# The operands of a Strassen MLP: residual rows turned by TensorE transposes, or read in short runs and turned in 32x32 blocks by VectorE

## The chip, the cores and the metric

One core of a Trainium2 chip. The metric is the device time of one execution in microseconds. Before the change its median over three runs is 1941.09 us (1940.94 to 1941.4).

## The reference

One layer of a decoder trunk with two mixers side by side, on 2048 tokens of 1024 features, float32 throughout. Cut to what matters:

```python
h  = rms_norm(x, attn_norm_g)
z  = h @ w_in                            # q, k, v, gate_b, gate_c, xc
y_attn = swa_sink_attention(rms_norm(q), rms_norm(k), v, sinks)   # window of 128
y_conv = gate_b * short_conv(gate_c * xc, conv_w)                 # 3 taps
x  = x + concat(rms_norm(y_attn), rms_norm(y_conv)) @ w_out
hm = rms_norm(x, mlp_norm_g)             # x / sqrt(mean(x^2) + eps) * g
x  = x + square(relu(hm @ w_up)) @ w_down        # 1024 -> 4096 -> 1024
```

The change is about `hm`: how the rows of the second `x` (called x1 in the kernel) become the operands of `hm @ w_up`.

## The kernel before, in words

**Numbers.** Each matrix operand is split into a high and a low part of a narrower float type (`F32R`), and each product is three matmuls (`mm3`, L264 to L266): high by high, high by low, low by high. A matmul contracts over the 128 partitions, so the features of `hm` must lie on the partitions, and the tokens along the row. The rows of x1 have tokens on the partitions. They have to be turned.

**Stages.** The mixers run in four chunks of 512 tokens (`mixers`). Beside the attention of a chunk, other work is issued step by step from a generator (`besides`): the convolution, the convolution half of the output projection (`out_projection` with half 1; its PSUM tiles are `pout`), and the preparation of the next chunk. The finished rows of x1 of each chunk are written to DRAM (`x1_dram`), and their factors 1/sqrt(mean + eps) stand in a small tile `rs_x1`, one column for 128 tokens. The attention half of the output projection of the last chunk comes last, in two halves of 512 columns (dh 0 and dh 1).

Then comes the MLP. It is one level of a Strassen scheme: the 1024 features and the tokens are cut in 2 x 2 blocks of 512, and seven products take the place of eight. Two token blocks are worked on: rows 0 to 1023 (token block 0) and rows 1024 to 2047 (token block 1). In each, four blocks b11, b21, b12, b22 (feature half, token half) and sums of them make the seven operands, which are kept in DRAM (`xop_dram[token block][product]`), 128 partitions by 2048 floats each. The order in which products read them is `ORDER` = 1, 2, 6, 5, 3, 7, 4. `load_x` reads an operand in two halves (L368), casts the high part on ScalarE (L369) and subtracts for the low part on VectorE (L370). The up projection's matmuls are L1401 (PSUM tile `u`), the down projection's L1508 (`d`). Up weights are loaded 8 products ahead (`PRE`), split by ScalarE and VectorE (`split_up`, L386 and L387, tile `wop`) 3 ahead (`LEAD`).

**First stage: the operands of token block 0.** `prepare_mlp` runs in `besides` of the last chunk, beside the attention, in place of the preparation of a next chunk. A tile is 128 tokens by 1024 features. For each of eight tiles, in the order of all four of the first token half and then all four of the second:

- `fetch`: one DMA of 128 rows into one of two `xt` buffers (L884), then `scaled` on VectorE: times the row's factor and times the gain row, which is a 128 x 1024 tile with the gain on all partitions (L280);
- `raised`: for each feature half, four TensorE transposes of 128 x 128 (L306) into a PSUM bank `tr`, and one copy of 128 x 512 from there to SBUF on ScalarE (L307);
- for a tile of the first token half, two stores to `xop_dram` (`x_put`, L313): operands 1 and 2; for one of the second, `x_sums`: a store for operand 3, and four subtractions on VectorE (L319) with a store each for operands 5, 6, 7 and 4.

So operands 1 and 2 are complete when the fourth tile is done. `begin_mlp` then reads operand 1, loads the first four up-weight blocks (`wu_first`, L381) and splits them. The matmuls of the MLP's first product follow in TensorE's order those of pout dh 0, and those of dh 1 come after them.

**Second stage: token block 1.** `prepare_rest` is a generator that takes one step after each MLP product of token block 0. Per tile: `fetch` (L1195), for the last chunk the row's factor (`norm_stats`), the row times its factor on VectorE (L1199); then four transposes (L1212) into `tr` and one VectorE multiplication from PSUM by the gain columns `g_cols` (L1216; features are on the partitions now, so the gain is a column); stores and subtractions as above, the subtractions on GpSimd.

**What sets the order.** The instructions of each engine run in an order that is fixed at build time. A scheduler arranges them by data dependences and by priorities: `ahead(n)` and the table `PRIO` raise the priority of a piece of work, and `FILL` says how many steps of `besides` go between pieces of attention. DMAs are issued by an engine's queue in its instruction order; nearly all loads and the `x_put` stores are issued by SyncE (SP), the stores of the MLP's hidden values by GpSimd (POOL) and ScalarE. An SP that waits for a buffer holds back what stands behind it.

Of the kernel before, what the change touches and what calls it, by code (L numbers as in the profile page):

```python
# [16 lines left out]
P = 128  # L17
# [53 lines left out]
STEPS = 3  # L71
REST = 7
# [29 lines left out]
def hymba_layer(  # L102
# [46 lines left out]
    ]  # L149
    wds_dram = [[dram.tile([P, 2, BW], F32, name=f"wds{g}_{i}") for i in range(2)] for g in range(NCG // 2)]  # L150
# [149 lines left out]
    def raised(xt, dst, name, tag="tr"):  # L300

        for k in range(2):
            pt = bank(tag, f"pt_{name}_{k}")
            for j in range(NB):
                r = slice((NB * k + j) * P, (NB * k + j + 1) * P)
                nc.tensor.transpose(pt[:, j * P : (j + 1) * P], xt[:, r], ident)  # L306
            nc.scalar.copy(dst(k), pt)  # L307
            yield

    def x_put(tb, t, i, b):  # L310

        dst = xop_dram[tb][ORDER.index(i)].rearrange("p (h t c) -> p h t c", h=2, t=NB)
        nc.sync.dma_start(dst[:, :, t], b.rearrange("p (h c) -> p h c", h=2))  # L313

    def x_sums(tb, t, b11, b21, b12, b22, t1):


        def sub(i, dst, a, b):
            nc.vector.tensor_tensor(dst, a, b, op=ALU.subtract)  # L319
            x_put(tb, t, i, dst)  # L320

        x_put(tb, t, 3, b22)
        sub(5, t1, b12, b11)
        sub(6, b11, b22, t1)
        sub(7, b12, b22, b12)
        sub(4, b21, b21, b11)

# [186 lines left out]
    with tc.tile_pool(name="mix_small", bufs=1) as mix_small, tc.tile_pool(name="mix", bufs=1) as mix:  # L514
# [321 lines left out]
        def out_projection(c, half, ys, rs, x1):  # L836

            for dh in range(2):
# [10 lines left out]
                for t, i in order:  # L849
# [11 lines left out]
                    with ahead(11):  # L861
# [3 lines left out]
                        if dh and not half:  # L865
# [5 lines left out]
                            if c + 1 < NCHUNK:  # L871
                                norm_stats(x1[t], f"m{c}_{t}", rs_x1[:, c * NT + t : c * NT + t + 1])
                    yield

        def prepare_mlp(gb):


            xs = [pool.tile([P, 8, CH], F32, tag=f"h{i}", name=f"xm{i}", bufs=1) for i in range(2)]
            xts = {}

            def fetch(t, i):
                r = i * CH + t * P
                xts[t, i] = row("xt", f"xt_m{i}_{t}", 2)
                nc.sync.dma_start(xts[t, i], x1_dram[r : r + P, :])  # L884
                with ahead(8):
                    scaled(xts[t, i], rs_x1[:, r // P : r // P + 1], gb)
# [661 lines left out]
```

## Time and profile before

| | before |
|---|---|
| median of 3 runs | 1941.09 us (1940.94 to 1941.4) |
| span of the profiled execution | 1937.4 us |
| TensorE (PE) busy | 1921.2 us, 99% of the span |
| VectorE (DVE) busy | 1192.2 us, 62% |
| ScalarE (ACT) busy | 836.8 us, 43% |
| GpSimd (POOL) busy | 270.1 us, 14% |
| matmuls of the up and down projection | 617.0 and 609.4 us busy |
| MLP's first matmul | 691.66 us after the span's start |
| DMA | 211,162 packets, 409.63 MB |

The profile is of one execution. It gives a span, from the first to the last recorded instruction, and no device time for that execution; the span is 3.7 us below the median of the runs, so what lies around it is about that much.

How to read the rows that follow. In a row of the timeline the first number is the start, in us from the span's start, the second the time taken by the instructions of the row, then engine, line, operation, output <- inputs, shape, and how many; a bracket at the end tells how long the engine had been idle and what ended the wait. "SPq" is a DMA issue by SP: its time is that of issuing, not of the transfer. A row of the groups gives the count, then minimum, median and maximum of one instruction in ns, and the first and last start. A row of the windows gives the stretch, its length and the busy time with the number of instructions of PE, weight loads, DVE, ACT and POOL, then the granted clock of TensorE, the busy share of the DMA engines, and GB/s. The row of a DMA queue gives packets, MB and the share of the 16 DMA engines' time.

### The profile page before, as it was taken

The page shows a single profiled execution, that of the slowest core. Times are in us where ns is not written, and L with a number is a line of the kernel's source. Part 1 is how long each engine was busy: PE and PEld are TensorE (multiplying, and loading weights), DVE is VectorE, ACT ScalarE, POOL GpSimd, SP SyncE. Part 2 cuts the span into 40 slices and gives each one's busy share as a digit, 9 for nine tenths or more (in the row PEclk, how much of TensorE's full clock was granted, in tenths as well). Part 3 has the DMA queues.
Part 4 walks back from the last instruction along what each step waited for, and adds up shares of the span by engine and source line. Part 5 has one row for each costly group of instructions (what it writes and reads, how often), then busy time and mean ns, then how long its engine had stood idle before and what let it go on. Part 6 is the DMA issues. An engine that isn't in the chain of part 4 may idle for free. (4 is left out here: it accounts for less than half of the span.)

```text
span 1937.4 us, 24882 instructions
## 1 busy us (share of the span) xinstructions
PE 1921.2 (99%) x9089; PEld 1599.6 (83%) x9089; DVE 1192.2 (62%) x1864; ACT 836.8 (43%) x1593; POOL 270.1 (14%) x471
## 2 busy tenths in 40 slices
PE   9999999999999999999999999999999999999999
PEld 9888888887888788888878888888888888888887
DVE  4885657447456769777868766666544334458541
ACT  6564444335344436454555554554422333232320
POOL 2122212312221111222200111101000000100000
PEclk9999999999999999999999999999999999999999
DMA  9774854564473897666665544437964446766631
GB/s 325 276 282 130 329 192 174 201 234 152 186 276 136 271 310 255 215 219 211 212 219 201 179 158 147 162 123 301 370 217 145 149 161 230 264 234 213 206 135 55
DMA packets 211162, 409.63 MB, mean 211 GB/s; under 512 B 18392, under 2 KB 121824, under 8 KB 199264
## 3 DMA queue, kind: packets, MB, share of 16 engines
q1 hardware_dynamic: 182416, 332.52, 49.4%
q0 software_dynamic: 15360, 51.39, 6.9%
q10 hardware_dynamic: 13264, 24.13, 3.3%
q8 instruction: 72, 1.18, 0.2%
q14 instruction: 50, 0.41, 0.1%
HBM read 282.16 MB, written 125.83 MB: 211 GB/s over the span
## 5 line engine op out<-in xcount | busy, mean ns | idle before, releaser
L1401 PE MATMUL u<-op_x,wop 128*128 128x512 f32 x2688 | 617.0, 390 | 1.7 <-DVE wop L387 0.8
L1508 PE MATMUL d<-op_w,op_f 128*128 128x512 f32 x2688 | 609.4, 389 | 0.0
L1401 PEld LDWEIGHTS u<-op_x,wop 128*128 128x128 f32 x2688 | 502.5, 188 | 109.3 <-DVE wop L387 3.0
L1508 PEld LDWEIGHTS d<-op_w,op_f 128*128 128x128 f32 x2688 | 504.5, 188 | 104.8
L370 DVE TENSOR_TENSOR op_f<-op_f 128x1024 fp32r<-128x1024 f32 x112 | 136.9, 1224 | 231.0 <-ACT op_f L369 230.3
L369 ACT CAST op_f<-op_f 128x1024 fp32r<-128x1024 f32 x112 | 117.6, 1052 | 349.2 <-DMA op_f<-fop 348.6
L386 ACT CAST wop<-wu 128x512 fp32r<-128x512 f32 x156 | 96.3, 620 | 102.2 <-PE u L1401 98.2
L387 DVE TENSOR_TENSOR wop<-wu,wop 128x512 fp32r<-128x512 f32 x156 | 107.3, 689 | 38.2 <-DMA wu<-in_w_up_dram 20.1
L1131 POOL DMA_DIRECT2D fop<-s x96 | 52.5, 547 | 435.2 <-DVE s L1134 415.3
L1137 DVE TENSOR_TENSOR u<-u,u 128x512 f32<-128x512 f32 x128 | 87.7, 685 | 22.1 <-PE u L1401 22.1
L370 DVE TENSOR_TENSOR op_w<-raw,op_w 128x1024 fp32r<-128x1024 f32 x56 | 68.4, 1222 | 30.6 <-ACT op_w L369 30.4
L369 ACT CAST op_w<-raw 128x1024 fp32r<-128x1024 f32 x56 | 58.8, 1052 | 48.9 <-PE d L1508 24.5
L652 ACT ACTIVATE sc_b<-sc_b,ngm_b 128x128 f32<-128x128 f32 x128 | 49.6, 390 | 28.7 <-DVE ngm_b L649 28.7
L684 POOL TENSOR_SCALAR_AFFINE_SELECT pp_b<-pp_b 128x512 fp32r<-128x512 f32 x60 | 41.3, 700 | 117.0 <-ACT pp_b L677 63.5
L386 ACT CAST wop<-wu_s 128x512 fp32r<-128x512 f32 x64 | 39.4, 619 | 34.7 <-PE u L1401 32.0
L1350 POOL DMA_DIRECT2D wds<-raw x16 | 8.6, 536 | 324.4 <-DVE raw L1348 324.4
L1143 ACT ACTIVATE u<-u 128x512 f32<-128x512 f32 x64 | 40.4, 632 | 29.8 <-DVE u L1137 26.7
L264 PE MATMUL pout<-w_wo,yt_c 128*128 128x512 f32 x128 | 52.5, 410 | 0.0
L266 PE MATMUL pout<-w_wo,yt_c 128*128 128x512 f32 x128 | 51.9, 406 | 0.0
L265 PE MATMUL pout<-w_wo,yt_c 128*128 128x512 f32 x128 | 51.2, 400 | 0.0
L264 PE MATMUL pout<-w_wo,at_b 128*128 128x512 f32 x128 | 50.2, 394 | 0.2 <-DVE ms_b L746 0.2
L265 PE MATMUL pout<-w_wo,at_b 128*128 128x512 f32 x128 | 50.0, 390 | 0.2 <-DVE w_wo L247 0.2
(256 smaller groups left out, 3123.4 us busy)
## 6 DMA issues: line engine op xcount, KB each, us to landing
op_f<-fop SPq DMA_DIRECT2D x112, 512.0 KB, 4.2
raw<-in_w_down_dram SPq DMA_DIRECT2D x72, 512.0 KB, 4.0
wu<-in_w_up_dram SPq DMA_DIRECT2D x128, 256.0 KB, 3.3
w_wo<-wo SPq DMA_DIRECT2D x24, 1024.0 KB, 6.8
fop<-s POOLq DMA_DIRECT2D x96, 256.0 KB, 2.4
fop<-u ACTq DMA_DIRECT2D x64, 256.0 KB, 2.4
op_x<-xop SPq DMA_DIRECT2D x28, 512.0 KB, 6.8
w_q<-qkv SPq DMA_DIRECT2D x24, 512.0 KB, 6.0
```

What stands on the lines that cost most here:

```text
L264: nc.tensor.matmul(ps, st(0), mv(0), start=first, stop=False)
L265: nc.tensor.matmul(ps, st(0), mv(1), start=False, stop=False)
L266: nc.tensor.matmul(ps, st(1), mv(0), start=False, stop=last)
L369: nc.scalar.copy(op[:, 0], raw)
L370: nc.vector.tensor_tensor(op[:, 1], raw, op[:, 0].bitcast(F32), op=ALU.subtract)
L386: splits.append(nc.scalar.copy(hi, blk).ins)
L387: nc.vector.tensor_tensor(lo, blk, hi.bitcast(F32), op=ALU.subtract)
L652: nc.scalar.activation(sc[:, hd, :], sc[:, hd, :], AF.Exp, bias=ngm[:, hd : hd + 1], accum_out=den[:, hd : hd + 1])
L1131: eng.dma_start(fop_dram[tb][ORDER_DOWN.index(i)][n // 2][:, n % 2], b)
L1137: return nc.vector.tensor_tensor(dst, ps, b, op=ALU.add).ins
L1401: nc.tensor.matmul(pt, wops[i][:, a, k, :], xops[tb, p][k // 2][:, b, k % 2, :], start=p not in GOES_ON and k + j == 0, stop=k + j == NB + ...
L1508: nc.tensor.matmul(ps[tb][j], fs[tb][:, a, k, j * P : (j + 1) * P], w[:, b, k, :], start=first and p not in GOES_ON and k + n == 0, stop=l ...
```

## The change

The rows of x1 are read with features on the partitions, and turned by VectorE.

- A tile is now 128 features of each of the two feature halves by 512 tokens (`(jj, i)`: feature part jj, token half i), again 128 partitions by 1024 floats in an `xt` buffer. `load_turned` fills it with four DMAs, one for each group of 32 partitions. In each, partition i takes, for 16 blocks of 32 tokens and both halves, token 32q + i, 32 features in a row: 1024 runs of 32 floats, 128 B.
- `turned` has VectorE transpose 128 x 512 in 32 x 32 blocks, after which features lie on the partitions and tokens along the row. Then one `scalar_tensor_tensor` multiplies by the gain column and by the row factors, which now are needed as a row of 512 tokens on all partitions.
- For that, `rs_out` writes the factors of a chunk, which stand as columns, to `rs_dram` with a GpSimd DMA, and two DMAs broadcast them back to all partitions: `rs_rows` in the first stage, in the buffer that held the gain row, and `rs_rest` in the second, in one of the two `xt` buffers.
- `raised`, its ScalarE copies and the gain row go, as do `scaled` on the fetched rows and, in the second stage, the factor's pass (L1199). That is 64 transposes in each stage.
- The first stage's tiles are taken in another order: by feature parts, the two token halves in turn. An operand now gets a quarter of its features with each pair of tiles.
- `x_put` stores 512 floats in a row for each partition, and `load_x` hands the halves to the matmul as they are.
- In `prepare_rest`, the factors of the last chunk are worked out first, for all four groups of rows, before any tile is fetched.

```diff
-    def raised(xt, dst, name, tag="tr"):
-        for k in range(2):
-            pt = bank(tag, f"pt_{name}_{k}")
-            for j in range(NB):
-                r = slice((NB * k + j) * P, (NB * k + j + 1) * P)
-                nc.tensor.transpose(pt[:, j * P : (j + 1) * P], xt[:, r], ident)
-            nc.scalar.copy(dst(k), pt)
-            yield
-
-    def x_put(tb, t, i, b):
-        dst = xop_dram[tb][ORDER.index(i)].rearrange("p (h t c) -> p h t c", h=2, t=NB)
-        nc.sync.dma_start(dst[:, :, t], b.rearrange("p (h c) -> p h c", h=2))
...
+    def load_turned(xb, src, r0, jj):
+        for pg in range(4):
+            rows = src[r0 : r0 + BW].rearrange("(q i) (k c) -> i k q c", i=TS, k=2)
+            c0 = jj * P + pg * TS
+            nc.sync.dma_start(
+                xb[pg * TS : (pg + 1) * TS].rearrange("p (k q c) -> p k q c", k=2, c=TS), rows[:, :, :, c0 : c0 + TS]
+            )
+
+    def turned(xb, k, dst, g, rs_row):
+        nc.vector.transpose(dst, xb[:, k * BW : (k + 1) * BW])
+        nc.vector.scalar_tensor_tensor(dst, dst, g, rs_row, op0=ALU.mult, op1=ALU.mult)
+
+    def x_put(tb, jj, i, b):
+        nc.sync.dma_start(xop_dram[tb][ORDER.index(i)][:, jj * BW : (jj + 1) * BW], b)
...
+    def rs_out(c):
+        nc.gpsimd.dma_start(
+            rs_dram[c].rearrange("(t p) -> p t", p=P), rs_x1[:, c * NT : (c + 1) * NT]
+        )
...
     def load_x(tb, p):
         src = xop_dram[tb][ORDER.index(p)].rearrange("p (h k c) -> p h k c", h=2, k=2)
-        ops_ = [load_op(src[:, h], f"x{tb}_{p}_{h}", early=p in ORDER[:2]) for h in range(2)]
-        return [op.rearrange("p s k c -> p s (k c)").rearrange("p s (t k c) -> p s k t c", t=NB, k=2) for op in ops_]
+        return [load_op(src[:, h], f"x{tb}_{p}_{h}", early=p in ORDER[:2]) for h in range(2)]
...
-        def prepare_mlp(gb):
+        def prepare_mlp():
             xs = [pool.tile([P, 8, CH], F32, tag=f"h{i}", name=f"xm{i}", bufs=1) for i in range(2)]
+            rows = pool.tile([P, 2, BW], F32, tag="gb", name="rs_rows", bufs=1)
+            for i in range(2):
+                nc.sync.dma_start(rows[:, i], rs_dram[i].partition_broadcast(P))
...
-            def fetch(t, i):
-                r = i * CH + t * P
-                xts[t, i] = row("xt", f"xt_m{i}_{t}", 2)
-                nc.sync.dma_start(xts[t, i], x1_dram[r : r + P, :])
-                with ahead(8):
-                    scaled(xts[t, i], rs_x1[:, r // P : r // P + 1], gb)
-            tiles = [(t, i) for i in range(2) for t in range(NT)]
+            def fetch(jj, i):
+                xts[jj, i] = row("xt", f"xt_m{i}_{jj}", 2)
+                load_turned(xts[jj, i], x1_dram, i * BW, jj)
+            tiles = [(jj, i) for jj in range(NB) for i in range(2)]
...
+                bs = [xs[jj % 2][:, m] for m in range(5)]
                 with ahead(9):
-                    for _ in raised(xts[t, i], lambda k: b[2 * i + k], f"m{i}_{t}"):
-                        pass
+                    for k in range(2):
+                        turned(xts[jj, i], k, bs[2 * i + k], g_cols[:, NB * k + jj : NB * k + jj + 1], rows[:, i])
...
     def prepare_rest():
...
+        rs_out(c)
+        rows = pool.tile([P, 2, BW], F32, tag="xt", name="rs_rest", bufs=2)
+        for i in range(2):
+            nc.sync.dma_start(rows[:, i], rs_dram[2 + i].partition_broadcast(P))
+        def fetch(jj, i):
+            xb = pool.tile([P, D], F32, tag="xt", name=f"xt_r{i}_{jj}", bufs=2)
+            load_turned(xb, x1_dram, (2 + i) * BW, jj)
+            return xb
...
             for i in range(2):
                 for k in range(2):
-                    pt = bank("tr", f"pt_{nm}")
-                    for j in range(NB):
-                        nc.tensor.transpose(...)
-                    b[k, i] = piece("st", f"st_{nm}")
-                    nc.vector.tensor_tensor(pieces(b[k, i]), pieces(pt), g_cols[...].to_broadcast([P, NB, P]), op=ALU.mult)
+                    b[k, i] = piece("st", f"st_m{2 + i}_{jj}_{k}")
+                    turned(xb, k, b[k, i], g_cols[:, NB * k + jj : NB * k + jj + 1], rows[:, i])
                     yield
                     yield
-            if t + 1 < NT:
-                fetch(t + 1)
+                if not i:
+                    xb = fetch(jj, 1)
+                elif jj + 1 < NB:
+                    xb = fetch(jj + 1, 0)
```

More of the change, by code (lines that the diff above doesn't have):

```diff
@@ L71 @@
 STEPS = 3
+TS = 32
 REST = 7
@@ L149, in hymba_layer @@
     ]
+    rs_dram = [dram.tile([CH], F32, name=f"rs_dram{c}") for c in range(NCHUNK)]
     wds_dram = [[dram.tile([P, 2, BW], F32, name=f"wds{g}_{i}") for i in range(2)] for g in range(NCG // 2)]
@@ L902, in prepare_mlp @@
                 if i:
[L903 removed]
+                    x_sums(0, jj, *bs)
                 else:
[L905 to L906 removed]
+                    x_put(0, jj, 1, bs[0])
+                    x_put(0, jj, 2, bs[1])
                 yield
@@ L925, in besides @@
             else:
-                steps = prepare_mlp(gain_row(mlp_norm_g, "g_mlp"))
+                steps = prepare_mlp()
             for i, _ in enumerate(steps):
```

55 lines of the change are left out of this document (18 added, 37 removed).

## The prediction, made before the changed kernel had run

> **What bounds the kernel.** I read the page first, then the chain that ended last, then TensorE's rows around the two places where the change cuts.
>
> ```profile
> span 1937.4 us, 24882 instructions
> PE 1921.2 (99%) x9089; PEld 1599.6 (83%) x9089; DVE 1192.2 (62%) x1864; ACT 836.8 (43%) x1593; POOL 270.1 (14%) x471
> ```
> ```profile
> 1035.71 288.32 PE u L1401 x1270
> 1324.04 609.29 PE d L1508 x2688
> ```
> ```profile
> L1401 PE MATMUL u<-op_x,wop 128*128 128x512 f32 x2688 | 617.0, 390 | 1.7 <-DVE wop L387 0.8
> L1508 PE MATMUL d<-op_w,op_f 128*128 128x512 f32 x2688 | 609.4, 389 | 0.0
> ```
>
> TensorE (PE) sets the end: 99% busy, the chain is nothing but its matmuls from 1035.71 us on, and in all the MLP's first product it waits 1.7 us. Work taken from PE shortens the run, and every microsecond that PE waits lengthens it. The median of the runs, 1941.09 us, stands 3.7 us above this span; I add the sum to both.
>
> Next, what a transpose costs PE. L306 is the first stage's (token rows 0 to 1023), L1212 the second's.
>
> ```profile
> L306 PE MATMUL pt_m<-ident,xt_m x64: 270/272/330, 643.7 to 679.0; 128*128 128x128 f32 x64
> L1212 PE MATMUL pt_m<-ident,xt_m x64: 270/272/273, 774.6 to 929.2; 128*128 128x128 f32 x64
> ```
> ```profile
> 643.72 0.60 PE L306 MATMUL pt_m<-ident,xt_m 128*128 128x128 f32 x4
> 644.07 0.48 PE L264 MATMUL pout<-w_wo,yt_c 128*128 128x512 f32 x1
> 644.39 0.40 PE L265 MATMUL pout<-w_wo,yt_c 128*128 128x512 f32 x1
> 644.62 0.40 PE L266 MATMUL pout<-w_wo,yt_c 128*128 128x512 f32 x1
> ```
>
> The 272 ns are pipelined time, not cost. Starts tell the cost: the four take 0.35 us (643.72 to 644.07), and the matmul behind them 0.32 instead of 0.23, so a group of four costs 0.45 us. There are 16 groups in each stage: 16 x 0.45 = 7.2 us a stage, 14.4 in all, not 128 x 0.272 = 34.8.
>
> Last, the hand-over from the first stage to the MLP:
>
> ```profile
> 665.38 0.63 PE L306 MATMUL pt_m<-ident,xt_m 128*128 128x128 f32 x4 [1.09 <-DVE xt_m L280]
> 668.81 0.38 PE L744 MATMUL pa_b<-mean,o_b 128*128 128x1 f32 x2 [0.35 <-ACT xm L307]
> 691.43 0.39 PE L266 MATMUL pout<-w_wo,at_b 128*128 128x512 f32 x1
> 691.66 3.91 PE L1401 MATMUL u<-op_x,wop 128*128 128x512 f32 x15
> ```
> ```profile
> 661.20 0.33 SPq L368 DMA_DIRECT2D op_x<-xop  x1
> 684.24 0.60 SPq L368 DMA_DIRECT2D op_x<-xop  x1
> 684.93 2.06 SPq L381 DMA_DIRECT2D wu_first<-in_w_up_dram  x4
> ```
> ```profile
> 689.36 1.05 ACT L369 CAST op_x<-op_x 128x1024 fp32r<-128x1024 f32 x1 [7.19 <-DMA op_x<-xop]
> 690.31 1.18 ACT L386 CAST wop<-wu_first 128x512 fp32r<-128x512 f32 x2
> ```
>
> PE goes from the attention half of the output projection (pout) into the MLP's first product (L1401) without a gap, but narrowly: its operand's second half was issued at 684.24 and the first weight was ready at 690.31 + 0.62 = 690.9, 0.8 us before PE came. From that read's issue to a PE that may start are 6.7 us.
>
> **The change, part by part.** *Transposes gone from PE:* minus 7.2 us in each stage; in the first also the two idles above, 1.09 + 0.35 = 1.4. PE would reach the MLP at 691.66 - 7.2 - 1.4 = 683.1.
>
> *Order of the tiles.* Before, a tile was 128 tokens by all 1024 features, the four tiles that operand 1 needs came first, and half of it was read back at 661.20. Now a tile is 128 features (of both halves) by 512 tokens and the two token blocks alternate, so operand 1 is complete only with the seventh of eight tiles (the eighth adds to operands 3 to 7). In the order that the build gives SP, its two reads stand behind all eight fetches and all 28 stores, the last sums' too; the four wu_first loads and w_wo stand behind them. PE's order is as before: L1401 comes first after pout dh 0, and the 48 matmuls of dh 1 (10.9 us at 0.227), which could cover a wait, come after. So PE waits for the end of a chain on VectorE (DVE).
>
> *That chain.* DVE's order has, behind the addition for the last tile of pout dh 0 (a L862) and ahead of op_x's split, the last four tiles: 8 block transposes, 8 scalings and 10 subtractions, 26 instructions of 128x512.
>
> ```profile
> 681.42 1.28 DVE L319 TENSOR_TENSOR xm<-xm 128x512 f32<-128x512 f32 x2
> 683.76 0.74 DVE L862 SCALAR_TENSOR_TENSOR x<-pout,rc,x 128x512 f32<-128x512 f32 x1
> 684.42 0.74 DVE L862 SCALAR_TENSOR_TENSOR x<-pout,ra,x 128x512 f32<-128x512 f32 x1
> ```
> ```profile
> L1199 DVE TENSOR_SCALAR xt_m<-xt_m,rs_x x8: 743/753/1775, 752.7 to 894.3; 128x1024 f32<-128x1024 f32 x8
> ```
>
> Subtractions go at 1.28 / 2 = 0.64 us, scalings at 0.66 (L862's starts). A block transpose is nowhere in this trace: bounds are L1199's 0.753 / 2 = 0.38 us for 512 elements and a pass twice as slow as L319's, 1.28. I take 0.64, the row of the same size between two SBUF tiles. [...] So 683.1 + 0.66 + 26 x 0.64 = 700.4 us if no read is late.
>
> *The reads.* A fetch was one DMA of 128 rows; it is now four, of 1024 runs of 128 B each, 4096 in all.
>
> ```profile
> L884 SPq DMA_DIRECT2D xt_m<-x_dram x8: 319/332/685, 484.5 to 668.1; - x8
> DMA to landing us min/median/max: 3.1/5.4/7.5
> ```
> ```profile
> L313 SPq DMA_DIRECT2D xop<-xm x28: 512/516/1137, 646.1 to 683.7; - x28
> L313 SPq DMA_DIRECT2D xop<-st_m x28: 513/519/881, 776.3 to 942.1; - x28
> ```
> ```profile
> q1 hardware_dynamic: 182416, 332.52, 49.4%
> ```
>
> One issue costs SP 0.33 us for rows and 0.52 for L313's finer pattern; I take 0.52, so a fetch 2.1 in place of 0.33. In the 2 us from 14 us on, when only constants of 4-byte runs moved:
>
> ```profile
> q1 hardware_dynamic: 1981, 0.02, 55.7%
> ```
> ```profile
> 13.16 1.22 SPq L1043 DMA_DIRECT2D g_cols<-in_mlp_norm_g_dram  x1
> ```
>
> that is 0.557 x 16 x 2 / 1981 = 9 ns for a tiny packet; the page's mean is 0.494 x 16 x 1937.4 / 182416 = 84 ns for 1823 B. In between, 128 B come to 14 ns, and a fetch to 4096 x 14 / 16 = 3.6 us of all 16 engines, against 1.5 for rows. With the landing median of 5.4 after the last issue: the seventh fetch stands on SP behind the second sums' stores, which DVE has at its fifth of the 26, 683.8 + 5 x 0.64 = 687.0; issued by 689.1, landed 694.5; DVE wants it after twelve, at 691.5. It waits 3.0. The eighth is issued by 692.2, landed 697.6, wanted at 698.3: no wait. DVE ends at 703.4.
>
> *The tail.* On op_x's reads:
>
> ```profile
> DMA to landing us min/median/max: 3.8/6.8/12.6
> ```
>
>  The 6.7 above hold 5.1 of that (684.24 to the cast at 689.36). Last store 0.52, first op_x read 0.4, then the 6.7 above: 703.4 + 0.5 + 0.4 + 6.7 = 711.0. PE starts the MLP at 711.0 instead of 691.7: 19.3 us later, 28 us idle. ACT's 16 copies (L307) go; it was waiting anyway. Behind the start the queues stand as before and move along.
>
> *First-stage rest.*
>
> ```profile
> 480.00:540.00 60.00, 60.00 (x333) 51.45 (x332) 35.05 (x68) 24.09 (x63) 14.03 (x22) 1.00 0.48 179
> ```
> ```profile
> L1131 POOL DMA_DIRECT2D fop<-s x96: 539/542/637, 757.3 to 1328.0; - x96
> ```
> ```profile
> L280 DVE SCALAR_TENSOR_TENSOR xt_m<-xt_m,rs_x,g_mlp x8: 1267/1284/1650, 496.8 to 674.7; 128x1024 f32<-128x1024 f32 x8
> ```
>
> The first two fetches and the two factor rows (which replace the gain row) are issued between 484 and 540, where PE is busy 60.00 of 60 and DMA 0.48: ten issues, 5 us of SP, hidden by weights loaded ahead; uncovered, w_qkv would be late by that. The small stores of the row factors on POOL (512 runs of 4 B; bounds 0.54 us, L1131's issue, and 1.22, L1043's) fall on an engine 14% busy: nothing; uncovered, each would delay the next halo copy by that. Up to pout dh 0's last addition DVE has 22 of its new or kept instructions, 22 x 0.64 = 14 us, where six L280 and 16 subtractions took 18: not late there. Operand layout in the matmul is now 512 in a row; no row tells strided from plain apart, u's 390 ns and d's 389 being equal: nothing.
>
> *Second stage.* DVE's work:
>
> ```profile
> L1216 DVE TENSOR_TENSOR st_m<-pt_m,g_cols x16: 673/680/683, 775.6 to 929.7; 128x512 f32<-128x512 f32 x16
> ```
> ```profile
> 700.00:950.00 250.00, 249.41 (x1130) 205.77 (x1129) 196.66 (x290) 130.36 (x216) 59.50 (x86) 1.00 0.70 234
> ```
> ```profile
> 963.56 1.70 SPq L368 DMA_DIRECT2D op_x<-xop  x2
> ```
>
> 16 x 0.68 + 8 x 0.75 = 17 us become 32 x 0.64 = 20.5, where DVE has 53 us free. The row factors now hold one of two xt buffers, so each fetch waits for the transposes of the one before, and SP with it; DVE's order leaves some 16 instructions (10 us) between them, a fetch needs 2.1 + 5.4 = 7.5. The last store was issued at 942.1, 21 us ahead of the operand's first read. Cost nothing, gain the 7.2 us. If that cover is gone, w_up's loads behind the fetch on SP are late next, and PE waits a few microseconds a fetch.
>
> **Sum:** + 19.3 - 7.2 = + 12.1 us; span 1949.5, time 1953.2.
>
> **Rivals.** *Short runs cost double* (the last fetches arrive late). A fetch takes 7.2 us of DMA, landing 9.0 instead of 5.4; the seventh arrives 3.6 later and the chain grows by as much: 1957. With issues of 1.22 (L1043) too, 4.9 a fetch, seventh and eighth each come some 5 later: to 1968. Against it: 9 ns for 4-byte runs. [...]
>
> *The second stage starves* (one buffer). For: SP's order mixes w_up's loads with the fetches. If each of eight fetches stalls PE 2 us: 1953 + 16 = 1969.
>
> *Faster: a transpose costs PE its 0.272 us.* Then the second stage gives 17.4 us and PE arrives 10 us sooner in the first, which draws DVE's chain with it: + 9 - 17 = - 8, 1933. It decides from about 0.24 us each, where both sides cancel; the starts above give 0.11.
>
> *No change to speak of:* DVE passes at 0.38 throughout, no read late, tail a microsecond shorter: 683.8 + 9.9 + 0.9 + 5.7 = 700.3, + 8.6 - 7.2 = + 1.4: 1942.5.
>
> *The change doesn't free PE* in the second stage, because other engines pace it: + 19: 1960. PE at 249.4 of 250 speaks against.
>
> **Numbers.** Forecast 0.60 (own range 1946 to 1960: lower end transposes 0.38, no wait, - 2.1 - 3.0 and 1.3 less landing, op_x's 5.1 here against 3.8 at best); short runs 0.14; starving 0.10; PE not freed 0.04; no change 0.06; faster 0.06. Slower than 0.2% (3.9 us, about what this kernel's runs can tell) 0.88, within 0.06, faster 0.06. Range 1945 to 1968.
>
> **What would show it.** Right: no matmul on xt_m; one PE idle of 20 to 30 us before the first L1401, ended by op_x's load or cast; transposes near 0.64 us; PE from there to the end 7 us shorter. Wrong: no such idle; fetches landing over 9 us; PE idles ended by wop between 770 and 950.

## The result and the profile after

The changed kernel takes 1970.54 us (median of 4 runs, 1969.17 to 1970.88) against 1941.24 beside it: a ratio of 1.0146, 95% interval 1.0132 to 1.0160. It is 29.3 us slower. The forecast was 12.1 us slower, 1953 us, with a range up to 1968: the direction and the place were right, the size was not.

From the page of the changed kernel: its span, the busy times, and the row of the up projection. Below that, the rows of the up and of the down projection's matmuls with their first and last starts: after (L1404, L1511), then before (L1401, L1508).

```profile
span 1969.2 us, 24719 instructions
PE 1916.1 (97%) x8961; PEld 1595.4 (81%) x8961; DVE 1212.6 (62%) x1896; ACT 827.1 (42%) x1577; POOL 275.0 (14%) x475
L1404 PE MATMUL u<-op_x,wop 128*128 128x512 f32 x2688 | 620.5, 393 | 38.9 <-ACT wop L396 34.7
```
```profile
L1404 PE MATMUL u<-op_x,wop x2688: 387/389/796, 717.5 to 1355.7; 128*128 128x512 f32 x192
L1511 PE MATMUL d<-op_w,op_f x2688: 388/389/389, 1355.9 to 1964.9; 128*128 128x512 f32 x192
```
```profile
L1401 PE MATMUL u<-op_x,wop x2688: 387/389/506, 691.7 to 1323.6; 128*128 128x512 f32 x192
L1508 PE MATMUL d<-op_w,op_f x2688: 388/389/389, 1323.9 to 1932.9; 128*128 128x512 f32 x192
```

The idle time ahead of the MLP's matmuls went from 1.7 to 38.9 us. The down projection is the same: 613 us from its first matmul to the end in both. So the loss lies in two stretches: up to the MLP's first matmul (691.7 before, 717.5 after: 25.8 us) and from there to the first down matmul (632.2 us before, 638.4 after: 6.2 us). Their sum, 32.0, is the spans' difference, 31.8. The medians differ by 29.3. The profiled execution of after took 1970.88 us with a span of 1969.2, so 1.7 us lie around a span; by that, the profiled execution of before, whose own time is not on record, took some 1939.1 us (an estimate) and was a quick one.

The waits of TensorE in the MLP, from its timeline (the bracket is the idle time before a row and what ended it):

```profile
685.63 0.39 PE L268 MATMUL pout<-w_wo,at_b 128*128 128x512 f32 x1
717.52 5.89 PE L1404 MATMUL u<-op_x,wop 128*128 128x512 f32 x13 [31.50 <-ACT wop L396]
...
761.78 44.23 PE L1404 MATMUL u<-op_x,wop 128*128 128x512 f32 x182 [3.22 <-ACT wop L396]
809.35 253.49 PE L1404 MATMUL u<-op_x,wop 128*128 128x512 f32 x1102 [3.33 <-DVE wop L397]
```

One idle stretch of 31.5 us between pout dh 0 and the MLP, as forecast (27.9), and two of 3.2 and 3.3 us behind it, which were not. The 13 matmuls behind the long one take 5.7 us until the next begins (717.52 to 723.25), where 13 at 0.227 us from start to start are 3.0. The windows show why; the column behind POOL's is the granted clock:

```profile
690.00:717.00 27.00, 0.00 (x0) 0.00 (x0) 14.69 (x23) 2.14 (x3) 0.00 (x0) 0.50 0.99 272
718.00:722.00 4.00, 4.00 (x10) 2.82 (x10) 2.61 (x5) 1.24 (x2) 0.00 (x0) 0.50 1.01 418
725.00:730.00 5.00, 5.00 (x24) 4.14 (x23) 0.87 (x2) 4.54 (x6) 0.00 (x0) 1.00 0.51 189
762.00:765.00 3.00, 3.00 (x8) 2.32 (x9) 3.00 (x5) 3.00 (x5) 0.00 (x0) 0.50 1.01 405
810.00:813.00 3.00, 3.00 (x9) 2.32 (x8) 2.16 (x4) 0.00 (x0) 1.08 (x2) 0.50 0.67 153
```

Behind each of the three idle stretches TensorE runs at half clock for some microseconds: 10 matmuls in 4 us at 0.50, 24 in 5 us at 1.00. In the long stretch itself the clock is 0.50 too (690 to 717).

### The profile page after: what moved, and what is told of

Read it like the earlier page. It is cut to its first block, busy times and chain, and to the rows that moved or that the text cites. A ratio compares the mean times of both kernels' runs of the same rounds, so it can differ in the third digit from the quotient of the medians.

```text
span 1969.2 us, 24719 instructions
## 1 busy us (share of the span) xinstructions
PE 1916.1 (97%) x8961; PEld 1595.4 (81%) x8961; DVE 1212.6 (62%) x1896; ACT 827.1 (42%) x1577; POOL 275.0 (14%) x475
## 4 chain that ended last, share of the span: by engine, by line
PE 84%; issue 5%; DMA 5%; DVE 3%; POOL 2%; ACT 1%; SPq 1%; POOLq 0%; DVEq 0%; ACTq 0%
PE d L1511 31%; PE u L1404 24%; PE pout L266 2%; PE pout L267 2%; PE pout L268 2%; PE pz L266 2%; PE pz L267 2%; PE pz L268 2%; PE pc_c L268 1%; PE px_c L266 1%; PE px_c L268 1%; PE px_c L267 1%; PE pc_c L266 1%; PE pc_c L267 1%; PE psc_b L645 1%
## 5 line engine op out<-in xcount | busy, mean ns | idle before, releaser
L1404 PE MATMUL u<-op_x,wop 128*128 128x512 f32 x2688 | 620.5, 393 | 38.9 <-ACT wop L396 34.7
L1404 PEld LDWEIGHTS u<-op_x,wop 128*128 128x128 f32 x2688 | 509.3, 190 | 149.6 <-ACT wop L396 35.6
L1511 PE MATMUL d<-op_w,op_f 128*128 128x512 f32 x2688 | 609.4, 389 | 0.0
L1511 PEld LDWEIGHTS d<-op_w,op_f 128*128 128x128 f32 x2688 | 504.7, 188 | 104.6
L397 DVE TENSOR_TENSOR wop<-wu,wop 128x512 fp32r<-128x512 f32 x156 | 111.1, 713 | 37.4 <-DMA wu<-in_w_up_dram 20.1
L380 ACT CAST op_w<-raw 128x1024 fp32r<-128x1024 f32 x56 | 58.8, 1052 | 43.7 <-PE d L1511 20.3
L380 ACT CAST op_x<-op_x 128x1024 fp32r<-128x1024 f32 x28 | 29.2, 1047 | 72.3 <-DMA op_x<-xop 72.2
L266 PE MATMUL pout<-w_wo,at_b 128*128 128x512 f32 x128 | 50.1, 394 | 0.2 <-DVE x L872 0.2
```

The lines of the kernel that those rows point to most:

```text
L266: nc.tensor.matmul(ps, st(0), mv(0), start=first, stop=False)
L380: nc.scalar.copy(op[:, 0], raw)
L397: nc.vector.tensor_tensor(lo, blk, hi.bitcast(F32), op=ALU.subtract)
L1404: nc.tensor.matmul(pt, wops[i][:, a, k, :], xops[tb, p][k // 2][:, b, k % 2, :], start=p not in GOES_ON and k + j == 0, stop=k + j == NB + ...
L1511: nc.tensor.matmul(ps[tb][j], fs[tb][:, a, k, j * P : (j + 1) * P], w[:, b, k, :], start=first and p not in GOES_ON and k + n == 0, stop=l ...
```

## What the second stage lost

The wait that ends at 809.35 is the end of a short chain. First GpSimd, then VectorE, in the changed kernel:

```profile
798.30 0.85 POOL L335 DMA_DIRECT2D rs_dram<-rs_x  x1 [0.29 <-POOL rs_x L191]
799.15 1.08 POOL L1140 DMA_DIRECT2D fop<-s  x2
808.00 0.69 DVE L1143 TENSOR_TENSOR s<-f,u 128x512 f32<-128x512 f32 x1 [7.42 <-DMA fop<-s]
808.61 0.68 DVE L397 TENSOR_TENSOR wop<-wu,wop 128x512 fp32r<-128x512 f32 x1
```

The row factors of the last chunk go out (rs_dram, 512 runs of 4 B); the hidden values' stores (fop) are issued right behind. VectorE needs a buffer that one of these stores must free, and waits 7.4 us. The next weight's split (wop, L397) stands behind it, so TensorE waits. For the eight microseconds the DMA rows read, in the window and by queue (packets, MB, share of 16 engines):

```profile
800.00:808.00 8.00, 6.01 (x27) 4.65 (x25) 0.58 (x2) 1.25 (x2) 1.29 (x3) 1.00 1.15 99
```
```profile
q0 software_dynamic: 236, 0.78, 114.2%
fop<-s POOLq DMA_DIRECT2D x2, 256.0 KB, 11.3
```

All DMA engines are busy while only 99 GB/s move. A packet of GpSimd's queue takes on average 1.142 x 16 x 8 / 236 = 619 ns, where the page of before gives 0.069 x 16 x 1937.4 / 15360 = 139 ns; a store of hidden values lands after 11.3 us in place of 2.4. The row factors' own packets are not the slow ones: from 799 to 800 us the queue shows 20 packets with 18.4% of the 16 engines, 147 ns each, and from 801 to 802, when packets of the hidden values start, 67 with 389.3%, 930 ns each (a packet's whole time is counted where it starts). So what suffers is the stores behind the one in 4-byte runs.

**rest_only: the change in the second stage alone.**

```diff
-        def prepare_mlp():                 # the first stage, its order and its layout as before the change
+        def prepare_mlp(gb):
...
     def x_put(tb, jj, i, b):
+        if tb == 0:                        # before's layout for token block 0, and load_x to match
```

> The change in the second stage alone (token block 1); the first stage, its order of tiles and its operand layout are those of before. Theory (the row factors' store stands on GpSimd's DMA queue ahead of the hidden values' stores): the 64 transposes give 7.2 us, one TensorE wait of about 3.3 us near 780 us, ended by wop, and half clock behind it cost 3.3 + 2.7: 1941.2 - 7.2 + 6.0 = 1940.0. The MLP starts at about 691.7 as before and the first 13 of its matmuls take 3.0 us. Rival 1 (the second stage is hidden, as predicted): no wait over 1 us, 1934. Rival 2 (the single xt buffer starves SP): several waits, one for each fetch, 1945 or more.

Measured: 0.9995 of before (0.9982 to 1.0008), where the theory's 1940.0 on 1941.2 is 0.9994. TensorE's wait is there, at the place and of the size that the theory gave:

```profile
779.35 3.07 PE L1424 MATMUL u<-op_x,wop 128*128 128x512 f32 x7 [3.63 <-DVE wop L414]
L1424 PE MATMUL u<-op_x,wop x2688: 387/389/632, 694.6 to 1322.7; 128*128 128x512 f32 x192
```

From the MLP's first matmul to the down projection it takes 628.3 us (1322.9 - 694.6) where before took 632.2. It is no starving by the one buffer: there is one wait of this kind, not one a fetch.

**rest_rs_act and rest_rs32: the same kernel, with the store moved or made coarser.**

```diff
-        nc.gpsimd.dma_start(rs_dram[c].rearrange("(t p) -> p t", p=P), ...)
+        nc.scalar.dma_start(rs_dram[c].rearrange("(t p) -> p t", p=P), ...)     # rest_rs_act
+        nc.gpsimd.tensor_copy(a[:, :NT], rs_x1[:, c * NT : (c + 1) * NT])       # rest_rs32
+        nc.vector.transpose(b, a)                                               # 128 x 32
+        for q in range(4):
+            nc.gpsimd.dma_start(dst[q], b[q * TS : q * TS + NT])                # runs of 32 floats
```

> The change in the second stage alone, and the row factors' store to DRAM issued by ScalarE in place of GpSimd. Theory (the wait of 3.3 to 3.6 us near 780 to 809 us is that of the hidden values' stores, which stand behind the row factors' store on GpSimd's queue and hold the buffers that VectorE writes next): the wait goes, though the row factors land as late as before and SP still waits for them; against the kernel before the full 7.2 us are won, a ratio of 0.9963. Rival (SP, which waits 12.5 us for the row factors ahead of the weight loads, is what makes wop late): the wait stays at 3 us or more, ratio 0.999.

> The change in the second stage alone, and the row factors turned by VectorE first, so that they go out in runs of 32 floats (four GpSimd DMAs of 4x32) in place of 512 runs of 4 B. Theory: the store lands in some 3 us in place of 9.5, both GpSimd's queue and SP's wait get shorter, and TensorE's wait goes: ratio 0.9963 as with ScalarE's queue. Rival (neither queue, but the one xt buffer is the cause): the wait stays, 0.999.

Moving it to ScalarE's queue was a miss: 0.9992 (0.9980 to 1.0004), no better than rest_only. Behind the store, which is issued at 770.5, TensorE's largest wait shrinks to 1.4 us (at 822.74; 3.4 us of half clock follow it), and another of 1.9 us, at 734.66, stands ahead of the store. But VectorE still waits for the hidden values' stores, 1.5 us and 3.1 us (the row shown), and SP 13.6 us for the row factors:

```profile
781.59 0.69 DVE L1163 TENSOR_TENSOR s<-u,s 128x512 f32<-128x512 f32 x1 [3.06 <-DMA fop<-s]
```

So it isn't the queue's order alone. With the 4-byte store on another queue, GpSimd's stores of the hidden values still land after 6.1 us (median from 766 to 782 us), where they need 2.5 in the same stretch of rest_rs32. SP's wait makes weights late too: at 787.74 VectorE waits 4.1 us for one. How much each of the two costs, this run doesn't separate. Runs of 32 floats cure both: 0.9965 (0.9953 to 0.9978), 1935.57 us against 1943.02 beside it, **faster than both kernels**. In its trace no TensorE wait over 0.3 us is left between 740 and 1020, the row factors' stores land after 4.0 us (median; 9.6 in the changed kernel), SP waits 6.9 us for them (12.7 in rest_only), and the up projection is

```profile
L1429 PE MATMUL u<-op_x,wop x2688: 387/389/504, 693.2 to 1318.3; 128*128 128x512 f32 x192
L1536 PE MATMUL d<-op_w,op_f x2688: 388/389/389, 1318.5 to 1927.6; 128*128 128x512 f32 x192
```

1318.5 - 693.2 = 625.3 us, 6.9 less than before. The forecast's price of 64 transposes, 7.2, stands.

**after_rs32: the same store in the whole changed kernel.**

> The changed kernel (both stages) with the row factors turned by VectorE and stored in runs of 32 floats. Theory (the 3.3 us wait near 809 us and the half clock behind it come from that store): both go, from the MLP's first matmul to the down projection's first it takes 632.5 us in place of 638.4, and the time is 1964.5, a ratio of 1.012 to before. Rival: the wait stays where the first stage has disturbed the order anyway, 1970.

Measured: 1.0081 (1.0066 to 1.0096) in place of 1.0146. That is some 12 us less, where 6 were expected. The wait near 809 and its half clock are gone, and they were the expected 6: 3.3 us of waiting and 3.0 lost to the clock. The profiled executions differ by 11.9 us. Of these, 3.4 lie in the MLP's start (714.1 for 717.5), 2.6 of them from before the first stage; and from there to the down projection it takes 630.0 us in place of 638.4, 8.4 less: those 6, and some 2 because the half clock behind the other two waits also ended sooner (at 717.3 and 761.7). The wait near 758 is still there, with 3.4 us.

**dummies: TensorE kept busy in the first stage's wait.**

```diff
+                if not half and dh and c + 1 == NCHUNK:
+                    for _ in range(136):
+                        nc.tensor.matmul(idle, ident, ident, start=True, stop=True)
```

> The changed kernel with 136 idle matmuls of 128x128 on the identity, into a spare PSUM bank, in TensorE's order between pout dh 0 and the MLP's first matmul (about 30 us at 0.22 each), so that TensorE isn't idle in the wait. Theory (the granted clock falls to 0.5 in an idle TensorE and comes back some 5.5 us after work starts): the first 13 matmuls of the MLP take 3.0 us in place of 5.9, and the time falls by 2.9 to 1967.6. Rival (the first matmuls are slow because operands arrive late, not by the clock): 13 matmuls in 5.9 us as in the changed kernel, 1970.5.

Measured: 1968.32 us, 1.0132 (1.0115 to 1.0149); against the changed kernel's 1.0146 that is 2.7 us less. The intervals overlap, and that it comes near the expected 2.9 is luck: the MLP's first 13 matmuls still take 5.3 us (718.30 to 723.63) and not 3.0. From the MLP's first matmul to the down projection's it takes 635.4 us in place of 638.4, with a wait of 1.8 us ahead of 760.8 that no half clock follows, and one of 3.9 ahead of 806.3. The clock, in windows of this kernel:

```profile
690.00:716.00 26.00, 26.00 (x235) 26.00 (x235) 13.75 (x22) 0.50 (x1) 0.00 (x0) 1.00 0.95 265
719.80:722.80 3.00, 3.00 (x8) 2.32 (x9) 1.59 (x3) 0.56 (x1) 0.00 (x0) 0.50 1.02 427
761.00:764.00 3.00, 3.00 (x14) 2.30 (x14) 3.00 (x5) 3.00 (x5) 0.00 (x0) 1.00 1.03 420
```

It stays at 1.00 while the idle matmuls run, where the changed kernel has 0.50. But the last of them ended at 716.7, 1.6 us ahead of the MLP's first at 718.3, and the clock fell at 719.7 even so. So the idle stretch is the cause of the half clock in it, and a wait far below 3 us was enough in one place and not in another: behind the 1.6 us ahead of 718.3, with 0.3 more at 719.4, the clock fell, behind the 1.8 ahead of 760.8 it did not (1.00 from 761 to 764).

## What made the first stage late

**first_only: the change in the first stage alone.**

> The change in the first stage alone (token block 0); the second stage and its operand layout are those of before. Theory: everything that the change lost is here but for the GpSimd stall: the MLP starts some 26 us late after 31 us of idle TensorE (less up to 3 us by which the profiled run of after was late before the first stage), the half clock costs 2.9, the wait near 758 us 2.6 and the clock behind it 2.5; the second stage's 7.2 us are not won: 1941.2 + 22.4 + 2.9 + 5.1 = 1971.6. Rival (the wait near 758 us belongs to the second stage's new loads): that wait is as in before, 0.6 us, and the time is 1966.5.

Measured: 1.0132 (1.0111 to 1.0152), 1968.58 against 1943.34: 25 us. On a before of 1941.2 that is 1966.8, the rival's number (1966.5). The MLP starts at 716.4. The wait near 758 us is 0.86 us here, as the rival had it; in the changed kernel it was 3.22, with the dummies 1.82, and with the stores moved (puts_act, below) there was none. What sets its size stays open.

The chain, in the changed kernel: some of SP's fetches and the first operand's read, VectorE's third tile and its last ones, ScalarE's cast. Rows between those shown are left out.

```profile
649.62 5.03 SPq L307 DMA_DIRECT2D xt_m<-x_dram  x4
...
682.44 2.71 SPq L307 DMA_DIRECT2D xt_m<-x_dram  x4
...
695.06 3.82 SPq L307 DMA_DIRECT2D xt_m<-x_dram  x4
708.09 0.92 SPq L379 DMA_DIRECT2D op_x<-xop  x2
```
```profile
667.74 0.70 DVE L313 STREAM_TRANSPOSE xm<-xt_m 128x512 f32<-128x512 f32 x1
...
696.58 1.30 DVE L313 STREAM_TRANSPOSE xm<-xt_m 128x512 f32<-128x512 f32 x2 [2.15 <-DMA xt_m<-x_dram]
701.60 1.30 DVE L313 STREAM_TRANSPOSE xm<-xt_m 128x512 f32<-128x512 f32 x2 [1.22 <-DMA xt_m<-x_dram]
706.21 1.44 DVE L324 TENSOR_TENSOR xm<-xm 128x512 f32<-128x512 f32 x2 [0.68 <-DMA xop<-xm]
```
```profile
714.71 2.24 ACT L380 CAST op_x<-op_x 128x1024 fp32r<-128x1024 f32 x2 [39.41 <-DMA op_x<-xop]
```

The four tiles behind pout dh 0 end on VectorE at 707.65 (forecast 703.4); from the first operand read at 708.1 the cast starts 6.6 us later and TensorE at 717.5 (forecast 711.0).

**after_rows: whole rows read in place of short runs.**

```diff
-        for pg in range(4):
-            nc.sync.dma_start(xb[pg * TS : (pg + 1) * TS]..., rows[:, :, :, c0 : c0 + TS])
+        nc.sync.dma_start(xb, src[r : r + P, :])
```

> The changed kernel with each fetch read as one DMA of 128 whole rows in place of four of 32-float runs; what VectorE turns is then not the block that it should be, so the output is not the reference's. Theory (VectorE's chain and the order of the tiles set the MLP's start, the short reads add only the three waits of 2.2, 1.2 and 0.7 us in the last tiles): the MLP starts some 4 us sooner, near 713.5, and the time is 1966.5. Rival (the short reads, with their four issues of 0.7 us or more on SP and their packets, pace the stage): it starts before 708, and the time is 1960 or less.

Measured: 1960.24 us, 1.0085 (1.0070 to 1.0100), the rival's number. The edit reads whole rows in both stages, and the blocks that VectorE turns are then not the operands'. The MLP starts at 685.1, 32 us sooner, but 17 us of the loss stay: TensorE waits 8.3 us for additions on VectorE and 11.3 for wop. The fetches themselves, from 640 to 700 us, with rows and (second fence) in the changed kernel:

```profile
L305 SPq DMA_DIRECT2D xt_m<-x_dram x6: 319/319/320, 647.6 to 673.5; - x6
DMA to landing us min/median/max: 3.7/4.7/5.8
```
```profile
L307 SPq DMA_DIRECT2D xt_m<-x_dram x24: 562/672/2997, 649.6 to 698.0; - x24
DMA to landing us min/median/max: 2.8/3.8/5.2
```

The short runs themselves are not late: each of a fetch's four DMAs (128 KB) lands 3.8 us after its own issue (median), the one of whole rows (512 KB) after 4.7. But the four issues take SP 2.7 to 5.0 us a fetch in place of 0.32, so that a fetch is there some 6 to 8 us after its first issue (an estimate from these rows), and they change the order that is built. In the changed kernel the third tile's fetch was issued by 654.7 and, at the longest landing of 5.2, was there by 659.9; VectorE turns it at 667.74, having waited in between for other engines' work that its order puts ahead (with rows the third tile is turned at 658.4). So part of the delay is the built order and not the reads. The rest is what VectorE waits behind pout dh 0, 2.15 + 1.22 + 0.68 = 4.1 us.

**prio and pool_subs: VectorE's order and VectorE's load.**

```diff
-                with ahead(9):
+                with tc.high_priority(offset=300):          # prio: transposes and scalings first
...
-            nc.vector.tensor_tensor(dst, a, b, op=ALU.subtract)
+            nc.gpsimd.tensor_tensor(dst, a, b, op=ALU.subtract)   # pool_subs: the first stage's 16
```

> The changed kernel with a higher priority (offset 300) for the first stage's transposes and scalings, so that the scheduler puts them ahead of other work in VectorE's order; reads, tiles and stores as in the changed kernel. Theory (VectorE's order, not the reads, put the chain late: with whole rows the order came out 20 us earlier): the MLP's first matmul before 703 and a time of 1956 or less, with some waits of TensorE before it on VectorE. Rival (four issues and a landing of 3.7 us for each of eight fetches into two buffers pace the stage): first matmul after 710, 1964 or more.

> The changed kernel with the first stage's 16 subtractions of 128x512 on GpSimd in place of VectorE. Theory (what stands on VectorE behind pout dh 0 sets the start): ten of the 26 instructions go, some 6 us, and GpSimd's last four cost 2 us more than VectorE's: the MLP starts at about 713, 1966. Rival (the reads pace the chain): the start stays within 2 us of 717.5, 1970.

Both miss in the start that they expected. prio: 1.0150 (1.0131 to 1.0168). Its new order puts a weight load of the output projection on SP behind fetches and stores, and TensorE waits 21 us for it:

```profile
693.72 0.41 SPq L235 DMA_DIRECT2D w_wo<-wo  x1
```
```profile
701.05 0.80 PE L267 MATMUL pout<-w_wo,yt_c 128*128 128x512 f32 x1 [20.99 <-DMA w_wo<-wo]
```

pool_subs: 1.0125 (1.0108 to 1.0142), an interval that overlaps the changed kernel's. By that the time is near the theory's 1966 (1965.5 on a before of 1941.24), but the MLP starts at 718.1, as the rival had it. VectorE's part of the chain ends at 702.9, 4.8 us sooner, but the last four subtractions then take GpSimd from 702.29 to 707.90, so SP's stores of them, and operand 1's read behind the stores (708.3, in the changed kernel 708.1), are no earlier.

The starts here and below are each from one profiled execution, and these come to the stage at different times: the first matmul of pout that starts at 541.86 in the changed kernel starts at 539.3 in after_rs32 and at 547.3 in prio. Differences of a few microseconds between starts say little.

**halves, h_34, hbp150: the old order of the tiles, with operand 1 read early.**

```diff
-            tiles = [(jj, i) for jj in range(NB) for i in range(2)]
+            tiles = [(jj, i) for i in range(2) for jj in range(NB)]
...
+                if n == 3:
+                    xops[0, 1] = load_x(0, 1)     # behind the fourth tile; weights with it (halves),
+                                                  # a tile later (h_34), or on GpSimd's queue (hbp150)
```

> The changed kernel with the first stage's tiles in the old order (all four of token half 0, then all four of half 1) and operand 1's two reads, with two of the four first weight loads, issued on SP right behind the fourth tile's stores; turning by VectorE stays in both stages. Theory (the order of the tiles and the place of the reads on SP make the late start, not the work on VectorE): TensorE goes into the MLP within 3 us of the end of pout dh 0, near 689 us, no half clock; 1970.5 - 28 - 2.9 = 1940, up to 1950 if operands 6 and 5, which now end the chain, come later. Rival (VectorE's chain and the short reads are too slow for the stage in any order): the MLP starts after 700 us, or as long a wait comes at the third product; 1955 or more.

> The changed kernel with the first stage's tiles in the old order, operand 1's reads behind the fourth tile's stores and the first weight loads behind the fifth's; the weights of the output projection stand ahead of them on SP. Theory (order and place of the reads make the late start): TensorE has no wait over 5 us before the MLP; operand 6, which now ends the chain near 715, is wanted 33 us after the MLP's start, at about 725, so nothing waits for it; 1970.5 - 31.5 - 2.9 = 1936 to 1942, so about as fast as before or up to 0.3% faster. Rival (VectorE's chain is too long for the stage in any order): a wait of over 10 us stays, before the MLP or at its third product, 1950 or more.

> All that the runs point to at once: row factors in runs of 32 floats; the first stage's tiles in the old order, its subtractions on GpSimd, a priority of 150 for transposes and scalings, operand 1 read behind the fourth tile's stores, the first weight loads on GpSimd's queue. Theory (order, queue places and VectorE's order are what made the MLP late): the first matmul before 692, no half clock, 1937 or less, a ratio of 0.9975 or less. Rival (VectorE can't do it in the time that it has): TensorE's waits before or in the MLP's first three products sum to 10 us or more, 1945 or more.

All three miss: 1.0167, 1.0153 and 1.0124 (1.0107 to 1.0141; the last one also holds the coarser row factors, which gave 0.6 per cent in after_rs32, the subtractions on GpSimd and a higher priority). In each an idle stretch of 22 to 30 us is back ahead of the MLP or in pout: 30.2 us for w_wo (halves), 22.1 for the first weights (h_34), 22.6 for w_wo (hbp150).

**puts_act, fetch_act, hp_act: SP relieved.** All have the coarser row factors.

```diff
-        nc.sync.dma_start(xop_dram[tb]..., b)
+        (nc.sync if tb else nc.scalar).dma_start(xop_dram[tb]..., b)     # puts_act; hp_act with the old order too
...
-            nc.sync.dma_start(xb[pg * TS : ...], rows[...])
+            (eng or nc.sync).dma_start(xb[pg * TS : ...], rows[...])      # fetch_act: eng = nc.scalar in the first stage
```

> The changed kernel with row factors in runs of 32 floats, and the first stage's 28 stores issued by ScalarE in place of SP; fetches stay on SP. Theory (SP is the path: a fetch stands behind stores that wait for VectorE, and VectorE then waits for the fetch): fetches go out as soon as a buffer is free, and the MLP's first matmul is 8 us or more ahead of the 714 of the same kernel with stores on SP, so before 706, and 1951 or less. Rival (a fetch itself, four issues and its landing, or VectorE's order sets the pace): first matmul within 3 us of 714, 1957 to 1960.

> The changed kernel with row factors in runs of 32 floats, and the first stage's fetches (four DMAs of 1024 short runs each) issued by ScalarE in place of SP; stores stay on SP. Theory (the issue of the short reads, 0.67 us in the median and up to 4 us for one of four, fills SP where 0.33 us for a whole fetch stood before): the first matmul before 706 and 1951 or less, if ScalarE, 7% busy behind 680, takes the issues without making attention late. Rival (the planner's order of VectorE or the landing sets the pace): within 3 us of 714.

> Row factors in runs of 32 floats, the first stage's stores on ScalarE's queue, tiles in the old order (token half 0 first) and operand 1's reads behind the fourth tile. Theory (SP's queue and the order together are what is late): TensorE's waits between 640 us and the MLP's third product sum to 10 us or less, 1944 or less. Rival (weights of the output projection are again late on SP, or VectorE's chain): one wait of over 15 us stays, 1955 or more.

puts_act: 1.0096 (1.0081 to 1.0111), the MLP at 717.0; fetch_act: 1.0071 (1.0054 to 1.0087), at 713.3; hp_act: 1.0106 (1.0091 to 1.0122), with 28.5 us of waiting for w_wo. after_rs32, which they start from, is at 1.0081. All three theories miss, and the starts and the long wait are those of their rivals. The wait only changes its place. In fetch_act ScalarE is stuck in issues, and attention waits for it:

```profile
687.53 16.36 ACTq L307 DMA_DIRECT2D xt_m<-x_dram  x11
703.93 0.30 ACT L713 CAST vz<-z 128x128 fp32r<-128x128 f32 x1 [15.78 <-DMA xt_m<-x_dram]
```

What follows: the one long idle stretch comes with the short reads (with whole rows it is gone, though 17 us of the loss stay), but not from their speed in the DMA engines. In puts_act, from 694 to 698 us, SP's queue shows

```profile
q1 hardware_dynamic: 2371, 0.30, 48.9%
```

that is 0.489 x 16 x 4 / 2371 = 13.2 ns for 128 B, where the forecast put 14. What is left, argued and not shown by itself, is that each fetch is four issues, through one queue that also carries the stores and the weights in between, into two buffers; and that the order is built around them. How much belongs to the built order and how much to the issues, the runs don't separate: every change of one also moved the other.

## Why the prediction was right and wrong

*Transposes gone from TensorE, 7.2 us a stage and 8.6 in the first:* right. Second stage 6.9 (rest_rs32). In the first, the same matmul of pout before the stage starts at

```profile
537.75 0.40 PE L264 MATMUL pout<-w_wo,at_b 128*128 128x512 f32 x1
```
```profile
541.86 0.40 PE L266 MATMUL pout<-w_wo,at_b 128*128 128x512 f32 x1
```

before and after, 4.1 us late, and the last of pout dh 0 at 691.43 and 685.63, 5.8 early: 9.9 won. The 4.1 us had come up before the stage, more than half of them in the first 25 us, and such lateness differs from one profiled execution to the next.

*The order of the tiles, the place of the reads on SP, one idle of TensorE ended by the first weight:* right in mechanism. Idle 31.5 us for 27.9: VectorE's end came 21.6 us behind TensorE's arrival (707.65 - 686.0) for 20.3, and the tail took 9.9 (707.65 to 717.52) for 7.6, as the operand landed in 6.6 us and not 5.1. The prices were good: a transpose (696.58 to 697.81 for two) 0.615 us for 0.64, a 128-B packet 13.2 ns for 14, the last fetches waited for 3.4 us in place of 3.0. One size was off: a fetch's issue is 2.7 to 5.0 us of SP, not 2.1; its landing of 3.8 us behind the last issue, for 5.4, paid that back.

*"The small stores of the row factors ... fall on an engine 14% busy: nothing":* **this step failed.** GpSimd's issue was priced (0.54 to 1.22, measured 0.85), the transfer was not, nor what waits for GpSimd's other stores. The 512 runs of 4 B slowed the stores behind them from 139 to 619 ns a packet, and through VectorE's buffers TensorE by 3.3 us. I had set dearer short runs aside by the 9 ns of a 4-byte run. But those 9 ns came from loads. Loads of 128 B took no more than was put here (13.2 ns, where 14 were put between 9 for 4 B and 84 for 1823 B); of the store to DRAM, the rows from 799 to 808 us show what became of the stores behind it, and why was not shown.

*What a wait costs:* the second step that failed, and the larger one. The half clock stands nowhere in the sum: each wait was priced with its own length. Behind 31.5, 3.2 and 3.3 us of idle, TensorE ran at half clock until 723.2, 767.6 and 815.3 (from the means of the windows there): 5.7, 5.8 and 6.0 us, half of which, 8.7 us, is lost.

*"Second stage: cost nothing, gain 7.2":* so the gain was there and lost again. From the MLP's first matmul to the down projection, 6.2 us more and not 7.2 less, 13.4 us off: half clock 8.7, the wait at 809 3.3, that at 758 2.6 above its 0.6 of before, together 14.6, so these three are all of it and a microsecond more. In the profiled executions the forecast fell short by 31.8 - 12.1 = 19.7 us. Of that, 13.4 lie here, 4.1 came up before the stage, and 717.5 - 4.1 - 711.0 = 2.4 are the first stage's own. In the medians it fell short by 17.2. None of the rivals was this one: "the second stage starves" put it to the one buffer, and its waits at every fetch are not there.

*Time around the span:* 1.7 us in the changed kernel, not 3.7. The median of before was set against what seems a quick profiled execution.

## What to carry to other kernels

Ask of every new DMA not only who issues it but which way it goes and in what runs: 2 KB in runs of 4 B into DRAM held up the stores behind them for some 8 us, while loads in runs of 128 B took 13.2 ns a run. When work is taken from the engine that sets the end, look at what it was ordered by: here 14 us of matmuls were won, and the order of tiles and one queue gave back more; the half of the change that was behind a long stretch of other work (the second stage), with its small store in coarser runs, is worth 0.35%. And price a wait of TensorE with the half clock that may stand behind it: 5.8 and 6.0 us of it behind waits of 3.2 and 3.3 us in the changed kernel, none behind 1.8 us in the run with dummies.

## What the runs showed of the hardware

The granted clock fell some microseconds into each of the changed kernel's three waits, not at their start. In finer windows it falls within

```profile
688.80:689.20 0.40, 0.00 (x0) 0.00 (x0) 0.40 (x1) 0.00 (x0) 0.00 (x0) 0.81 0.00 0
760.60:760.90 0.30, 0.00 (x0) 0.00 (x0) 0.27 (x1) 0.30 (x1) 0.00 (x0) 0.71 0.80 328
808.40:808.80 0.40, 0.00 (x0) 0.00 (x0) 0.40 (x2) 0.00 (x0) 0.00 (x0) 0.64 0.28 10
```

which by their means puts the falls at 689.05, 760.73 and 808.51: 3.0, 2.2 and 2.5 us after the waits began (at 686.02, 758.56 and 806.02). Waits of 3.2 and 3.3 us were enough; in the run with dummies 1.6 us (716.7 to 718.3, and 0.3 at 719.4) were, in rest_rs_act 1.4 (ahead of 822.74), while 0.9 us (first_only) was not.

Nor does the length of a wait alone decide. In the run with dummies 1.82 us ahead of 760.79 left the clock at 1.00, in rest_rs_act 1.92 us ahead of 734.66 did, and each is longer than the single waits of 1.6 and 1.4 us above. What decides beside the length was not shown; and the lengths hang on the matmuls' ends, which are modelled.
